# The first product of the dense stage in quarter blocks, one behind each rotating product

## The chip, the cores and the metric

The kernel runs on one core of one Trainium2 chip, as one program and one launch. The metric is the device time of that core in microseconds (us), smaller is better. The engines go by the short names of the profile: PE is the matrix engine (its weight loads are PEld), DVE the vector engine, ACT the scalar engine, POOL the general-purpose engine, SP the engine that only issues DMAs here. Each engine works through its own queue in order. Work on different engines is ordered only by semaphores.

## What is computed

The reference is one encoder layer over 1024 tokens of width 1024: attention beside a convolution, an output product, and then a product-key expert layer with 128 x 128 = 16384 experts, of which each token uses 16 in each of 8 heads. Only that last layer matters here:

```python
u = peer_u[e]                                          # 128 experts of one token
h = jax.nn.gelu(jnp.einsum('cd,chkd->chk', xc, u))
return jnp.einsum('chk,chkd->cd', g * h, peer_v[e])
```

Products are in float32, made of three products each in a shorter format: every operand X is split into a high part (rounded) and a low part (the rest), and X·Y is taken as XhYh + XhYl + XlYh.

## The kernel before

**Two ways through the experts.** Three of the eight token tiles (384 tokens, "gathered") fetch their 768 x 128 expert rows by indirect DMA: one DMA a step (`Gather.issue`, L1147, POOL) brings one row of 1024 numbers to each of 128 tokens, and DVE either forms a dot product with it (phase 0, L1178) or adds it, weighted, to a running sum (phase 1, L1192). There are 768 such steps. The other five tiles (640 tokens, "dense") are multiplied with all 16384 experts, and a dense matrix of gates, zero nearly everywhere, chooses. The dense work goes in 128 blocks of 128 experts.

**A dense block i** has these parts:

- The first product: the block's U (512 KB, `uload`, L1209), split by `usplit` into `uh` on ACT and `ul` on DVE or POOL, times the tokens `HN`. That is 2 halves of 320 tokens, each 8 chunks x 3 = 24 matmuls of 320 columns (`uhalf`, L1479), into one PSUM bank, the tile `hps` (`ubank`). ACT takes the gelu of each half into `ho` (`ugelu`, L1489).
- 33 of the 128 blocks (`US`, index `UI`) have their first product made before the main loop. Their `ho` waits in DRAM (`HDm`) and is read back by `hload` (L1459). They are blocks 0, 1, 2, and then about every fourth. The other 95 blocks make it in the main loop.
- `amake`: DVE multiplies the two halves of `ho` by the gates `gl` (L1466), ACT rounds it to `ah` (L1469), DVE forms `al` (L1471). `gload` (L1442) fetches the gates for four blocks at a time, in two halves, into 3 buffers.
- `vload` (L1446) and `vsplit`: V to `vh` on ACT and `vl` on POOL (L117, L120).
- The second product: 10 output tiles of 128 tokens x 512. Four of them stay in PSUM for all blocks (`acc`, 12 matmuls of 512 columns a block). Six rotate: each is made every second block for two blocks at once (6 matmuls, tile `prot`, one PSUM bank), and DVE adds the bank to `X` (L1514). So a block has three rotations, 18 matmuls. PSUM is full: four banks `acc`, one `hps`, one `prot`, two for the gather's running sum `ga`.

**The order is written out by hand** (a manual schedule), so every engine's queue is in program order. Block i goes: some gather steps, `amake(i+1)`, loads, the four `acc` products, `vsplit(i+1)`, `usplit(i+3)`, and then the rotations. If block i+2 needs its first product (`hasu`), one half of it follows each of the first two rotations: rotation, 24 matmuls, rotation, 24 matmuls, rotation. If it doesn't (a "plain" block), the rotations follow one another, and the second of them borrows the bank `hps`. `wts` and `SPOTS` say how many gather steps a block has and where: a plain block gets 0.3 of the weight of another.

Of the kernel before, what the change touches and what calls it, by code (L numbers as in the profile page):

```python
# [8 lines left out]
F32 = mybir.dt.float32  # L9
# [5 lines left out]
ALU = mybir.AluOpType  # L15
# [5 lines left out]
P = 128  # L21
# [3 lines left out]
DC = D // P  # L25
# [6 lines left out]
NK = 128  # L32
# [6 lines left out]
NG = 3  # L39
# [1 line left out]
GCH = 4  # L41
NPERS = 4
K0 = 33
GW = 0.3
WIN = 2
NVI = 3
NO2 = 2
# [25 lines left out]
def peer_block(tc, I, out):  # L73
# [4 lines left out]
    def f(ap):  # L78
        return ap.bitcast(F32)
# [35 lines left out]
    def split(hi, lo, src, hi_eng=A, lo_eng=V):  # L115
        if hi_eng is A:
            A.copy(hi, src)  # L117
        else:
            hi_eng.tensor_copy(hi, src)
        lo_eng.tensor_tensor(lo, src, f(hi), op=ALU.subtract)  # L120
# [995 lines left out]
    class Gather:  # L1116
        def __init__(self):
            self.seq = [(ph, t, k) for t in range(NG) for ph in (0, 1) for k in range(P)]
            self.ni = self.nc = 0
            self.rows = {}  # L1120
            self.hh, self.aa = {}, {}
            self.limit = NG * 256
            self.slots = None
            self.ps = None
            self.hload = -1

        def h(self, t):
            h = QB[:, 0:2, :].rearrange("p a b -> p (a b)")
            if self.hload < t:
                SY.dma_start(h, HND[t])  # L1130
                self.hload = t
            return h

        def to_psum(self, ps):
            self.ps = ps
# [26 lines left out]
        def adv(self, n=1):  # L1162
            for _ in range(n):
                if not self.ready():
                    return
                self.fill()
                ph, t, k = self.seq[self.nc]
                r = self.rows.pop(self.nc)
                self.nc += 1
                ps = self.ps  # L1170
                if ph == 0:
                    h = self.h(t)
                    if k == 0:
                        self.hh[t] = gp.tile([P, P], F32, name=f"hh{t}")
                        if ps is not None:
                            A.copy(ps, h)
                    jk = QB[:, 2, :].bitcast(BF)
                    V.scalar_tensor_tensor(jk, r, 1.0, h if ps is None else ps, op0=ALU.mult, op1=ALU.mult,  # L1178
                                           accum_out=self.hh[t][:, k:k + 1])
                else:  # L1180
                    if k == 0:
                        aa = gp.tile([P, P], F32, name=f"aa{t}")
                        A.activation(aa[:], self.hh[t][:], AF.Gelu_apprx_tanh)
                        V.tensor_tensor(aa[:], aa[:], gg[t][:], op=ALU.mult)
                        self.aa[t] = aa
                    xt = X[:, t, :]
                    if k == 0 and ps is not None:
                        A.copy(ps, xt)
                    if k == P // 2 and t + 1 < NG:
                        self.h(t + 1)  # L1190
                    to = xt if ps is None else ps
                    V.scalar_tensor_tensor(to, r, self.aa[t][:, k:k + 1], to, op0=ALU.mult, op1=ALU.add)  # L1192
                    if k == P - 1 and ps is not None:
                        A.copy(xt, ps)
                self.slots.append(r)

    gat = Gather()
    US = sorted({0, 1, 2, *(int(2 + j * (NK - 2) / (K0 - 2)) for j in range(K0 - 2))})
# [13 lines left out]
    def HE(i):  # L1212
        return G if i in UI and UI[i] <= KM else A

    def usplit(i):
        raw = RAW.pop(("u", i))
        uh = uu.tile([P, DC, P], F32R, name="uh", tag="uh", bufs=2)
        ul = uu.tile([P, DC, P], F32R, name="ul", tag="ul", bufs=2)
        split(uh[:], ul[:], raw[:], hi_eng=HE(i), lo_eng=(G if UI[i] <= KM else V) if i in UI else G if i % 4 else V)
        UW[i] = (uh, ul)  # L1220

    def useg(i, hps, d0, d1):
# [185 lines left out]
    with ExitStack() as vs:  # L1408
# [40 lines left out]
        def vsplit(i):  # L1449
# [3 lines left out]
            split(vh[:], vl[:], raw[:], lo_eng=G)  # L1453
            CH[i] = (vh, vl)

        def hload(i):
            if i in UI:
                ho = vp.tile([P, TD], F32, name="ho", tag="ho", bufs=2)
                SY.dma_start(ho[:], HDm[UI[i]])  # L1459
                HO[i] = ho  # L1460

        def amake(i, mid=lambda: None):
            ho = HO.pop(i)
            for hf in range(2):
                o = ho[:, hf * HT_:(hf + 1) * HT_].rearrange("p (b t) -> p b t", t=TB)
                V.tensor_tensor(o, o, gl[i - i % GCH, hf][:, :, i % GCH, :], op=ALU.mult)  # L1466
            ah = vp.tile([P, TD], F32R, name="ah", tag="ah", bufs=WIN + 1)
            al = vp.tile([P, TD], F32R, name="al", tag="al", bufs=WIN + 1)
            A.copy(ah[:], ho[:])  # L1469
            mid()  # L1470
            V.tensor_tensor(al[:], ho[:], f(ah[:]), op=ALU.subtract)  # L1471
            AL[i] = (ah, al)

        def uhalf(i, hf, ps, d0=0, d1=DC):
            a, b = segs[hf]
# [12 lines left out]
            a, b = segs[hf]  # L1488
            A.activation(ho[:, a:b], ps[:, :b - a], AF.Gelu_apprx_tanh)  # L1489

        def loads(i, u):
            if 0 <= u < NK and u not in UI:
                uload(u)
            if 0 <= i < NK:
                if i % GCH == 0:
                    gload(i)
                hload(i)
                vload(i)

        last = [-1] * len(rot)  # L1500
        HP = {}
# [16 lines left out]
        gat.to_psum(ga[:])  # L1518
        for i in range(KM + 2, K0):
            uload(US[i])  # L1520
        loads(-1, 3)
        loads(0, -1)
        loads(1, -1)
        for i in range(KM, K0):
            if i + 1 < K0:
                usplit(US[i + 1])
            else:
                amake(0)
                vsplit(0)
            ho = vp.tile([P, TD], F32, name="hm", tag="al", bufs=WIN + 1)[:]  # L1530
            for hf in range(2):
                hps = ubank() if hf == 0 else psv.tile([P, 512], F32, name="prot", tag="r", bufs=1)
                uhalf(US[i], hf, hps)
                ugelu(ho, hf, hps)
            SY.dma_start(HDm[i], ho)

        def uof(i):
            return i + 2 < NK and i + 2 not in UI


        SPOTS = {True: (4, 3, 1, 4, 3, 2, 0, 4), False: (1, 2, 0)}
        gat0 = gat.nc
        wts = np.cumsum([(1.0 if uof(i) else GW) * (i < NK - GLAST) for i in range(NK)])
        for i in range(NK):
            nx = i + 1
            hasu = uof(i)
            ng = gat0 + int(np.ceil((ngat - gat0) * wts[i] / wts[-1])) - gat.nc
            gs = [0] * 6
            for j in range(ng):
                gs[SPOTS[hasu][j % len(SPOTS[hasu])]] += 1  # L1550
            if nx in HP:
                ugelu(HO[nx], 1, HP.pop(nx))
            gat.adv(gs[0])
            if nx < NK:
                amake(nx, lambda: gat.adv(gs[1]))
            else:
                gat.adv(gs[1])
            gat.adv(gs[2])
            loads(i + 2, i + 4)
            ah, al, vh, vl = *AL[i], *CH[i]  # L1560
            for j, (t, n) in enumerate(pers):
                mm3(acc[j][:], ah[:, t * P:(t + 1) * P], al[:, t * P:(t + 1) * P], vh[:, n:n + 512],
                    vl[:, n:n + 512], i == 0, i == NK - 1)
            if nx == NK:
                gat.adv(10000)
                gf = gat.slots.pop(0)
                SY.dma_start(gf, row("final_g"))
                for t in range(NG):
                    final(t)
                for j, (t, n) in enumerate(pers):  # L1570
                    V.tensor_tensor(X[:, NG + t, n:n + 512], X[:, NG + t, n:n + 512], acc[j][:], op=ALU.add)
                    if n:
                        final(NG + t)
            if nx < NK:
                vsplit(nx)
            if i + 3 < NK and i + 3 not in UI:
                usplit(i + 3)
            rs_ = [w for w in range(len(rot)) if i % WIN == w % WIN or i == NK - 1]
            if hasu:
                HO[i + 2] = vp.tile([P, TD], F32, name="ho", tag="ho", bufs=2)  # L1580
            for j, w in enumerate(rs_):
                rotate(w, i, not hasu and j % 2 == 1)
                if nx == NK and rot[w][1]:
                    final(NG + rot[w][0])
                gat.adv(gs[3 + j] if 3 + j < 6 else 0)
                if hasu and j < 2:
                    hps = ubank()
                    uhalf(i + 2, j, hps)
                    if j == 0:
                        ugelu(HO[i + 2], 0, hps)  # L1590
                    else:
                        HP[i + 2] = hps
            gat.adv(sum(gs[3 + len(rs_):]))
            CH.pop(i - WIN, None)
        while fq:
            final2()
    h_.close()
# [55 lines left out]
```

## Time and profile before

| | |
|---|---|
| median of three runs | 3069.0 us (3067.18 to 3072.01) |
| the profiled execution, its own time | 3063.84 us |
| span of the profiled execution | 3062.0 us |
| PE busy | 2807.3 us, 92% of the span |
| DVE / POOL / ACT busy | 2425.7 / 1901.2 / 1152.5 us (79 / 62 / 38%) |
| DMA, mean | 232 GB/s over the span; 323 GB/s from 1384 to 3037 us |

The page of the profile gives totals over the whole span. The dense loop, which the change touches, runs from the first matmul of block 0 (1384.04 us) to the first of block 127 (3036.99 us), a little over half of the span. A matmul's duration in the rows is longer than its share of the engine, because matmuls are pipelined. The pitch, from one start to the next, is what a matmul costs.

### The profile page before, as it was taken

The numbers are of one execution on the slowest core, as the hardware profiler recorded it, in microseconds if no ns is written. First come the engines' busy times: TensorE is split into PE (matmuls) and PEld (weight loads), VectorE is DVE, ScalarE is ACT, GpSimd is POOL, SyncE is SP. The second block draws the span as 40 slices with busy tenths as digits, with TensorE's granted clock in tenths as the row PEclk, the third lists the DMA queues.
The fourth block names the chain that finished last, engine by engine and source line by source line (L and its number), as shares of the span: only waits on it lengthen the run. The fifth ranks groups of instructions, "written<-read, shape, count | busy, mean of one in ns | idle before, by whom it ended". The sixth has DMA issues, their size and how long they took to land.

```text
span 3062.0 us, 44586 instructions
## 1 busy us (share of the span) xinstructions
PE 2807.3 (92%) x16048; PEld 2491.3 (81%) x16048; DVE 2425.7 (79%) x4496; ACT 1152.5 (38%) x2376; POOL 1901.2 (62%) x1526
## 2 busy tenths in 40 slices
PE   7878899799999999979999999999999999999998
PEld 6767788698988888858888888888888888888887
DVE  5889997458666977658888888888888888788877
ACT  3216565243577677662222222222222222222222
POOL 2578852105446666747777777777767676767765
PEclk8989999899999999989999999999999999999999
DMA  3111000153345666678989898989999898889985
GB/s 124 48 67 35 8 1 15 44 159 118 97 146 191 210 232 248 223 262 331 337 326 345 320 338 318 340 330 334 345 317 325 302 339 306 316 314 323 331 296 217
DMA packets 296719, 710.32 MB, mean 232 GB/s; under 512 B 25265, under 2 KB 135217, under 8 KB 296369
## 3 DMA queue, kind: packets, MB, share of 16 engines
q0 software_dynamic: 110592, 402.70, 35.7%
q1 hardware_dynamic: 156800, 252.85, 24.5%
q10 hardware_dynamic: 29104, 51.91, 4.5%
q8 instruction: 126, 2.06, 0.3%
q14 instruction: 97, 0.79, 0.1%
HBM read 640.46 MB, written 66.91 MB: 231 GB/s over the span
## 4 chain that ended last, share of the span: by engine, by line
PE 65%; DVE 19%; issue 6%; ACT 4%; DMA 3%; POOL 1%; ACTq 1%; SPq 0%; POOLq 0%; DVEq 0%
PE hps L1479 19%; PE prot L123 5%; PE hps L1227 5%; PE prot L124 5%; PE prot L125 5%; PE acc L123 3%; PE acc L124 3%; PE acc L125 3%; DVE y L147 3%; PE pg L1099 3%; DVE ul L120 2%; DVE QB L1178 2%; DVE ga L1192 1%; DVE ho L1466 1%; PE pq L282 1%
## 5 line engine op out<-in xcount | busy, mean ns | idle before, releaser
L1479 PE MATMUL hps<-HN,uh 128*128 128x320 f32 x3072 | 679.6, 309 | 5.4 <-ACT ho L1234 5.3
L1479 PEld LDWEIGHTS hps<-HN,uh 128*128 128x128 f32 x3072 | 522.7, 188 | 21.2 <-issue 5.5
L1147 POOL DMA_INDIRECT rows<-peer_u,ei x339 | 369.4, 1090 | 194.3 <-DVE QB L1178 126.9
L1479 PE MATMUL hps<-HN,ul 128*128 128x320 f32 x1536 | 475.3, 309 | 0.0
L1147 POOL DMA_INDIRECT rows<-peer_v,ei x329 | 339.2, 1031 | 216.3 <-DVE ga L1192 146.3
L1514 DVE TENSOR_TENSOR X<-X,prot 128x512 f32<-128x512 f32 x352 | 241.0, 685 | 238.1 <-PE prot L125 236.6
L1192 DVE SCALAR_TENSOR_TENSOR ga<-rows,aa,ga 128x1024 f32<-128x1024 f32 x329 | 422.4, 1284 | 5.2 <-DMA rows<-peer_v,ei 1.2
L123 PE MATMUL prot<-vh,ah 128*128 128x512 f32 x699 | 282.7, 404 | 84.3 <-DVE X L1514 84.1
L1489 ACT ACTIVATE ho<-hps 128x320 f32<-128x320 f32 x190 | 83.1, 437 | 728.0 <-PE hps L1479 728.0
L120 POOL TENSOR_TENSOR vl<-vr,vh 128x1024 fp32r<-128x1024 f32 x128 | 309.1, 2415 | 56.0 <-DMA vr<-peer_v 36.6
L1178 DVE SCALAR_TENSOR_TENSOR QB<-rows,ga 128x1024 bf16<-128x1024 f32 x271 | 329.4, 1216 | 5.6 <-DMA rows<-peer_u,ei 1.7
L1469 ACT CAST ah<-ho 128x640 fp32r<-128x640 f32 x128 | 93.3, 729 | 521.3 <-DVE ho L1466 307.6
L1479 PEld LDWEIGHTS hps<-HN,ul 128*128 128x128 f32 x1536 | 289.1, 188 | 0.0
L124 PE MATMUL prot<-vl,ah 128*128 128x512 f32 x699 | 277.9, 398 | 0.0
L125 PE MATMUL prot<-vh,al 128*128 128x512 f32 x699 | 276.5, 396 | 0.0
L120 POOL TENSOR_TENSOR ul<-ur,uh 128x1024 fp32r<-128x1024 f32 x96 | 240.2, 2503 | 2.6
L123 PEld LDWEIGHTS prot<-vh,ah 128*128 128x128 f32 x699 | 132.9, 190 | 121.0 <-DVE X L1514 100.1
L1109 ACT COPY gblk<-pg 128x128 f32<-128x128 f32 x640 | 175.6, 439 | 99.2 <-PE pg L1099 71.2
L1227 PE MATMUL hps<-HN,uh 128*128 128x320 f32 x992 | 210.5, 334 | 0.0
L124 PE MATMUL acc<-vl,ah 128*128 128x512 f32 x512 | 205.1, 401 | 3.4 <-POOL vl L120 3.4
L123 PE MATMUL acc<-vh,ah 128*128 128x512 f32 x512 | 206.1, 403 | 0.0
L125 PE MATMUL acc<-vh,al 128*128 128x512 f32 x512 | 203.9, 398 | 0.0
(265 smaller groups left out, 6672.9 us busy)
## 6 DMA issues: line engine op xcount, KB each, us to landing
ur<-peer_uT SPq DMA_DIRECT2D x128, 512.0 KB, 4.9
vr<-peer_v SPq DMA_DIRECT2D x128, 512.0 KB, 6.4
GD<-gblk ACTq DMA_DIRECT2D x80, 512.0 KB, 4.9
gl<-GD SPq DMA_DIRECT2D x64, 640.0 KB, 8.0
wqr<-peer_wq SPq DMA_DIRECT2D x32, 512.0 KB, 3.9
ho<-HDm SPq DMA_DIRECT2D x33, 320.0 KB, 6.3
HDm<-ho SPq DMA_DIRECT2D x31, 320.0 KB, 2.3
s<-SD SPq DMA_DIRECT2D x64, 128.0 KB, 2.4
```

What stands on the lines that cost most here:

```text
L120: lo_eng.tensor_tensor(lo, src, f(hi), op=ALU.subtract)
L123: PE.matmul(ps, ah, bh, start=start, stop=False)
L124: PE.matmul(ps, ah, bl, start=False, stop=False)
L125: PE.matmul(ps, al, bh, start=False, stop=stop)
L1109: A.copy(gblk[b][k][:, :, q * 4:q * 4 + 4].rearrange("p i t -> p t i"), pg[:, :, k * w:k * w + w])
L1147: G.indirect_dma_start(out=r, out_offset=None, in_=I["peer_v" if ph else "peer_u"], in_offset=bass.IndirectOffsetOnAxis(ap=ge[t][:, k:k + ...
L1178: V.scalar_tensor_tensor(jk, r, 1.0, h if ps is None else ps, op0=ALU.mult, op1=ALU.mult, accum_out=self.hh[t][:, k:k + 1])
L1192: V.scalar_tensor_tensor(to, r, self.aa[t][:, k:k + 1], to, op0=ALU.mult, op1=ALU.add)
L1227: PE.matmul(hps[:, j, :b - a], (uh, uh, ul)[st3][:, dc, :], HN[(0, 1, 0)[st3]][:, dc, a:b], start=dc == 0 and st3 == 0, stop=dc == DC - 1 ...
L1469: A.copy(ah[:], ho[:])
L1479: PE.matmul(ps[:, :b - a], (uh, uh, ul)[st3][:, dc, :], HN[(0, 1, 0)[st3]][:, dc, a:b], start=dc == 0 and st3 == 0, stop=dc == DC - 1 and ...
L1514: V.tensor_tensor(X[:, NG + t, n:n + 512], X[:, NG + t, n:n + 512], pr, op=ALU.add)
```

## The change

In the loop, the first products no longer belong to block i+2. A list `ulist` of the 95 blocks that need one is worked off in quarters: `ugroup` makes 4 of the 8 chunks of one half (12 matmuls of 320 columns), and one `ugroup` follows every rotation of every block. So 127 blocks with three each hold the 95 x 4 = 380 quarters. The gelu comes behind every second quarter. `uahead` splits a block's U ahead and issues the load of the one two further on. The four `acc` products are spread: one behind the first rotation, one behind the second, two behind the third. Every rotation uses `prot`; none borrows `hps`.

`amake` is cut into `amake1` (gates and `ah`) and `amake2` (`al`), and stands behind the second quarter instead of at the head of the block, with a share of the gather steps between. The gather steps are spread evenly, 5 or 6 in each block. `vsplit(i+1)` stands at the head of the block. In `usplit` all low parts but those of the first products ahead of the loop go to POOL; before, 31 of them in the loop went to DVE. `ho` gets three explicit buffers, of which one is the space `QB` that held the gather's token row; that row is loaded into a gather slot instead (`stage`), four steps ahead of its use. The last block stands behind the loop.

```diff
+        def stage(self, t):
+            if t not in self.staged:
+                self.staged[t] = self.slots.pop(0)
+                SY.dma_start(self.staged[t], HND[t])
...
-        split(uh[:], ul[:], raw[:], hi_eng=HE(i), lo_eng=(G if UI[i] <= KM else V) if i in UI else G if i % 4 else V)
+        split(uh[:], ul[:], raw[:], hi_eng=HE(i), lo_eng=V if i in UI and UI[i] > KM else G)
...
+        hfree = [vp.tile([P, TD], F32, name=f"ho{j}")[:] for j in range(2)]
+        hfree.append(QB[:, 0:2, :].rearrange("p a b -> p (a b)")[:, :TD])
...
+        def uahead():
+            m = ug["g"] // 4
+            if ug["split"] < min(m + 2, len(ulist)):
+                usplit(ulist[ug["split"]])
+                ug["split"] += 1
+                if ug["load"] < len(ulist):
+                    uload(ulist[ug["load"]])
+                    ug["load"] += 1
+
+        def ugroup():
+            m, q = divmod(ug["g"], 4)
...
+            i, (hf, d) = ulist[m], divmod(q, 2)
...
+            if d == 0:
+                ug["ps"] = ubank()
+            uhalf(i, hf, ug["ps"], d * DC // 2, (d + 1) * DC // 2)
+            if d == 1:
+                if hf == 0:
+                    HO[i] = hfree.pop(0)
+                ugelu(HO[i], hf, ug["ps"])
+            ug["g"] += 1
...
-            gat.adv(gs[0])
-            if nx < NK:
-                amake(nx, lambda: gat.adv(gs[1]))
...
-            loads(i + 2, i + 4)
...
+        SPOTS = (0, 2, 1, 0, 2, 2, 0)
...
+            hload(nx)
+            if len(hfree) > 1:
+                hload(i + 2)
+            loads(i + 2)
+            vsplit(nx)
+            uahead()
+            rs_ = [w for w in range(len(rot)) if i % WIN == w % WIN]
+            rotate(rs_[0], i, False)
+            accum(i, (0,))
+            ugroup()
+            gat.adv(gs[0])
+            rotate(rs_[1], i, False)
+            accum(i, (1,))
+            ugroup()
+            uready(nx)
+            amake1(nx)
+            gat.adv(gs[1])
+            amake2(nx)
+            rotate(rs_[2], i, False)
+            accum(i, (2, 3))
+            ugroup()
+            gat.adv(gs[2])
```

## Rows read from the trace of the kernel before

**Rows 1.** The page's chain of work that ended last, its shares of the span by engine.

```profile
PE 65%; DVE 19%; issue 6%; ACT 4%; DMA 3%; POOL 1%; ACTq 1%; SPq 0%; POOLq 0%; DVEq 0%
```

**Rows 2.** Busy time by stretch: the dense loop from the first matmul of block 0 to the first of block 127 (stretch, length, then busy us and instructions of PE, PEld, DVE, ACT, POOL, then the granted clock of PE as a share of full speed, the DMA share and GB/s), and under it two stretches of 100 us.

```profile
1384.04:3036.99 1652.95, 1569.91 (x8363) 1395.76 (x8362) 1393.20 (x1809) 395.73 (x552) 1176.50 (x886) 0.98 0.90 323
...
1700.00:1800.00 100.00, 95.33 (x519) 85.10 (x518) 86.11 (x92) 24.38 (x34) 71.74 (x56) 1.00 0.93 338
2900.00:3000.00 100.00, 94.06 (x482) 83.17 (x481) 80.72 (x86) 22.28 (x31) 67.46 (x50) 0.93 0.86 306
```

**Rows 3.** The timeline of PE in the dense loop (start us, duration us, engine, line, operation, names, count; in brackets the idle time before and what ended it): a block with a first product begins at 2255.68, the next block, a plain one, at 2269.57, and the one behind it at 2279.62.

```profile
2255.68 0.39 PE L123 MATMUL acc<-vh,ah 128*128 128x512 f32 x1
...
2259.76 0.45 PE L1479 MATMUL hps<-HN,uh 128*128 128x320 f32 x2
...
2260.20 0.46 PE L1479 MATMUL hps<-HN,uh 128*128 128x320 f32 x2
...
2269.57 0.39 PE L123 MATMUL acc<-vh,ah 128*128 128x512 f32 x1
...
2278.14 0.50 PE L123 MATMUL prot<-vh,ah 128*128 128x512 f32 x1 [2.97 <-DVE X L1514]
...
2279.62 0.40 PE L123 MATMUL acc<-vh,ah 128*128 128x512 f32 x1
```

**Rows 4.** What PE waited for in the dense loop (us in total, times, longest).

```profile
PE prot L123 <- DVE X L1514: 81.3, 33, 3.0
```

**Rows 5.** The timeline of DVE, and under it of POOL, across that plain block's idle stretch.

```profile
2274.29 3.19 DVE L120 TENSOR_TENSOR ul<-ur,uh 128x1024 fp32r<-128x1024 f32 x1
2277.41 0.68 DVE L1514 TENSOR_TENSOR X<-X,prot 128x512 f32<-128x512 f32 x1
2278.00 0.67 DVE L1514 TENSOR_TENSOR X<-X,hps 128x512 f32<-128x512 f32 x1
...
2274.01 2.38 POOL L120 TENSOR_TENSOR vl<-vr,vh 128x1024 fp32r<-128x1024 f32 x1
```

**Rows 6.** The timeline of PE behind another plain block's idle stretch.

```profile
2225.84 0.63 PE L123 MATMUL prot<-vh,ah 128*128 128x512 f32 x1
2226.26 0.63 PE L124 MATMUL prot<-vl,ah 128*128 128x512 f32 x1
```

**Rows 7.** Groups by line on DVE from 1386.6 to 3052 us (count, then busy us, mean ns of one, and the idle time before them with what ended it).

```profile
L1192 DVE SCALAR_TENSOR_TENSOR ga<-rows,aa,ga 128x1024 f32<-128x1024 f32 x329 | 422.4, 1284 | 5.2 <-DMA rows<-peer_v,ei 1.2 <-ACT ga L1188 0.5
L1178 DVE SCALAR_TENSOR_TENSOR QB<-rows,ga 128x1024 bf16<-128x1024 f32 x269 | 327.0, 1216 | 5.6 <-DMA rows<-peer_u,ei 1.7 <-ACT ga L1176 1.4
...
L1466 DVE TENSOR_TENSOR ho<-ho,gl 128x320 f32<-128x320 f32 x252 | 123.5, 531 | 2.4 <-DMA ho<-HDm 2.4
L1471 DVE TENSOR_TENSOR al<-ho,ah 128x640 fp32r<-128x640 f32 x126 | 103.1, 818 | 0.0
L120 DVE TENSOR_TENSOR ul<-ur,uh 128x1024 fp32r<-128x1024 f32 x31 | 101.6, 3279 | 0.0
L1192 DVE SCALAR_TENSOR_TENSOR ga<-rx,aa,ga 128x1024 f32<-128x1024 f32 x55 | 70.6, 1283 | 0.4
L1178 DVE SCALAR_TENSOR_TENSOR QB<-rx,ga 128x1024 bf16<-128x1024 f32 x45 | 54.7, 1216 | 3.6 <-DMA rx<-peer_u,ei 1.8 <-ACT ga L1176 1.4
```

**Rows 8.** One group by line on POOL in the same stretch, and the timeline of POOL: two gather steps with nothing between, and one beside a two-input operation of DVE.

```profile
L120 POOL TENSOR_TENSOR ul<-ur,uh 128x1024 fp32r<-128x1024 f32 x64 | 154.5, 2413 | 0.0
...
2266.42 0.95 POOL L1147 DMA_INDIRECT rows<-peer_v,ei  x1 [0.30 <-issue]
2267.68 0.94 POOL L1147 DMA_INDIRECT rows<-peer_v,ei  x1 [0.30 <-issue]
...
2272.73 1.27 POOL L1147 DMA_INDIRECT rows<-peer_v,ei  x1 [2.87 <-DVE ga L1192]
```

**Rows 9.** The timeline of DVE, and under it of POOL, at the start of the dense stage: two-input operations of DVE alone and beside a split on POOL.

```profile
1370.08 1.23 DVE L120 TENSOR_TENSOR ul<-ur,uh 128x1024 fp32r<-128x1024 f32 x1 [26.16 <-ACT uh L117]
...
1382.14 1.93 DVE L1466 TENSOR_TENSOR ho<-ho,gl 128x320 f32<-128x320 f32 x1
...
1381.32 2.41 POOL L120 TENSOR_TENSOR vl<-vr,vh 128x1024 fp32r<-128x1024 f32 x1 [36.59 <-DMA vr<-peer_v]
```

**Rows 10.** The timeline of SP behind a load of gates, what SP's queue waited for with that load, and the DMA view of one issue of `vr` each at 1664.47 and at 1871.07 (count, size, us from issue to landing).

```profile
1664.47 1.24 SPq L1446 DMA_DIRECT2D vr<-peer_v  x1
...
SPq L1442 <- DVE ho L1466: 302.6, 31, 15.8
...
vr<-peer_v SPq DMA_DIRECT2D x1, 512.0 KB, 7.1
...
vr<-peer_v SPq DMA_DIRECT2D x1, 512.0 KB, 10.6
```

**Rows 11.** The timeline of ACT in the dense loop.

```profile
1563.89 1.05 ACT L117 CAST vh<-vr 128x1024 fp32r<-128x1024 f32 x1
1564.84 1.04 ACT L117 CAST uh<-ur 128x1024 fp32r<-128x1024 f32 x1
1568.07 0.44 ACT L1489 ACTIVATE ho<-hps 128x320 f32<-128x320 f32 x1 [2.20 <-PE hps L1479]
```

**Rows 12.** The DMA view from 1400 to 3030 us (issues, KB each, median us to landing).

```profile
QB<-HND SPq DMA_DIRECT2D x2, 512.0 KB, 7.8
```

**Rows 13.** The timeline of PE at the end: the first matmul of block 127.

```profile
3036.99 0.40 PE L123 MATMUL acc<-vh,ah 128*128 128x512 f32 x1
```

More of the change, by code (lines that the diff above doesn't have):

```diff
@@ L43 @@
 K0 = 33
-GW = 0.3
 WIN = 2
@@ L1125, in __init__ @@
             self.hload = -1
+            self.staged = {}
         def h(self, t):
@@ L1171, in adv @@
                 if ph == 0:
-                    h = self.h(t)
+                    h = self.h(t) if ps is None else ps
                     if k == 0:
@@ L1175, in adv @@
                         if ps is not None:
-                            A.copy(ps, h)
+                            self.stage(t)
+                            A.copy(ps, self.staged[t])
+                            self.slots.append(self.staged.pop(t))
                     jk = QB[:, 2, :].bitcast(BF)
-                    V.scalar_tensor_tensor(jk, r, 1.0, h if ps is None else ps, op0=ALU.mult, op1=ALU.mult,
+                    V.scalar_tensor_tensor(jk, r, 1.0, h, op0=ALU.mult, op1=ALU.mult,
                                            accum_out=self.hh[t][:, k:k + 1])
@@ L1188, in adv @@
                         A.copy(ps, xt)
-                    if k == P // 2 and t + 1 < NG:
-                        self.h(t + 1)
                     to = xt if ps is None else ps
@@ L1195, in adv @@
                 self.slots.append(r)
+                if ph and k == P - 4 and t + 1 < NG and ps is not None:
+                    self.stage(t + 1)
     gat = Gather()
@@ L1454, in vsplit, with amake1 @@
             CH[i] = (vh, vl)
+        hfree = [vp.tile([P, TD], F32, name=f"ho{j}")[:] for j in range(2)]
+        hfree.append(QB[:, 0:2, :].rearrange("p a b -> p (a b)")[:, :TD])
         def hload(i):
[L1457 to L1463, printed above, removed]
+            if i in UI and i not in HO and i < NK:
+                HO[i] = hfree.pop(0)
+                SY.dma_start(HO[i], HDm[UI[i]])
+        def amake1(i):
+            ho = HO[i]
             for hf in range(2):
@@ L1467, in amake, with amake2 @@
             ah = vp.tile([P, TD], F32R, name="ah", tag="ah", bufs=WIN + 1)
+            A.copy(ah[:], ho)
+            AL[i] = ah
+        def amake2(i):
+            ho = HO.pop(i)
             al = vp.tile([P, TD], F32R, name="al", tag="al", bufs=WIN + 1)
[L1469 to L1472, printed above, removed]
+            V.tensor_tensor(al[:], ho, f(AL[i][:]), op=ALU.subtract)
+            AL[i] = (AL[i], al)
+            hfree.append(ho)
         def uhalf(i, hf, ps, d0=0, d1=DC):
@@ L1489, in ugelu, with loads @@
             A.activation(ho[:, a:b], ps[:, :b - a], AF.Gelu_apprx_tanh)
-        def loads(i, u):
-            if 0 <= u < NK and u not in UI:
-                uload(u)
+        def loads(i):
             if 0 <= i < NK:
@@ L1496, in loads, with uready @@
                     gload(i)
-                hload(i)
                 vload(i)
+        ulist = [i for i in range(NK) if i not in UI]
+        ug = dict(g=0, split=0, load=0, ps=None)
+        def uahead():
[8 more added lines that the diff above has]
+            m, q = divmod(ug["g"], 4)
+            if m >= len(ulist):
+                return
+            i, (hf, d) = ulist[m], divmod(q, 2)
+            if ug["split"] <= m:
+                uahead()
[4 more added lines that the diff above has]
+                if hf == 0:
+                    HO[i] = hfree.pop(0)
+                ugelu(HO[i], hf, ug["ps"])
+            ug["g"] += 1
+        def uready(i):
+            while i not in UI and ulist.index(i) >= ug["g"] // 4:
+                ugroup()
         last = [-1] * len(rot)
@@ L1520, in peer_block @@
             uload(US[i])
-        loads(-1, 3)
-        loads(0, -1)
-        loads(1, -1)
+        for j in range(2):
+            uload(ulist[j])
+        ug["load"] = 2
+        hload(0)
+        loads(0)
+        loads(1)
         for i in range(KM, K0):
@@ L1527, in peer_block @@
             else:
-                amake(0)
+                amake1(0)
+                amake2(0)
                 vsplit(0)
+                uahead()
             ho = vp.tile([P, TD], F32, name="hm", tag="al", bufs=WIN + 1)[:]
@@ L1535, in peer_block, with accum @@
             SY.dma_start(HDm[i], ho)
[L1537 to L1552, printed above, removed]
-            gat.adv(gs[0])
-            if nx < NK:
-                amake(nx, lambda: gat.adv(gs[1]))
-            else:
-                gat.adv(gs[1])
-            gat.adv(gs[2])
-            loads(i + 2, i + 4)
+        def accum(i, js):
@@ L1560, in peer_block @@
             ah, al, vh, vl = *AL[i], *CH[i]
-            for j, (t, n) in enumerate(pers):
+            for j in js:
+                t, n = pers[j]
                 mm3(acc[j][:], ah[:, t * P:(t + 1) * P], al[:, t * P:(t + 1) * P], vh[:, n:n + 512],
                     vl[:, n:n + 512], i == 0, i == NK - 1)
[L1564 to L1592, printed above, removed]
@@ L1593, in peer_block @@
-            gat.adv(sum(gs[3 + len(rs_):]))
-            CH.pop(i - WIN, None)
+        SPOTS = (0, 2, 1, 0, 2, 2, 0)
+        gat0 = gat.nc
+        nb = NK - GLAST
+        for i in range(NK - 1):
+            nx = i + 1
+            ng = gat0 + -(-(ngat - gat0) * min(nx, nb) // nb) - gat.nc
+            gs = [0] * 3
+            for j in range(ng):
+                gs[SPOTS[j % len(SPOTS)]] += 1
+            hload(nx)
[3 more added lines that the diff above has]
+            vsplit(nx)
+            uahead()
+            rs_ = [w for w in range(len(rot)) if i % WIN == w % WIN]
[12 more added lines that the diff above has]
+            accum(i, (2, 3))
+            ugroup()
+            gat.adv(gs[2])
+            CH.pop(i - WIN, None)
@@ new lines, in peer_block @@
+        accum(NK - 1, range(len(pers)))
+        gat.adv(10000)
+        gf = gat.slots.pop(0)
+        SY.dma_start(gf, row("final_g"))
+        for t in range(NG):
+            final(t)
+        for j, (t, n) in enumerate(pers):
+            V.tensor_tensor(X[:, NG + t, n:n + 512], X[:, NG + t, n:n + 512], acc[j][:], op=ALU.add)
+            if n:
+                final(NG + t)
+        for w in range(len(rot)):
+            rotate(w, NK - 1, w % 2 == 1)
+            if rot[w][1]:
+                final(NG + rot[w][0])
```

## The prediction

> **What bounds the kernel now.** I read the chain of waits first: PE holds 65% of it, DVE 19% [rows 1]. Busy time by stretch then shows that the dense loop is the place: there PE is busy 1569.91 of 1652.95 us, DVE 1393, POOL 1177, and the DMA engines stand at 0.90 [rows 2]. No engine is full, so I looked for where PE stands idle. In PE's timeline a block with a first product takes 2269.57 − 2255.68 = 13.89 us without a gap; the plain block behind it takes 10.05 us, of which 2.97 are idle [rows 3]. The list of waits says that this is the pattern: PE waits for DVE's add to X 33 times, 81.3 us in all [rows 4]. DVE's timeline says why the add is late: a `ul` of 3.19 us stands ahead of it [rows 5]. So PE bounds 95 blocks of the loop, and DVE the plain ones.
>
> How much can be won? The price of a matmul is its pitch. Three of 320 columns take 2260.20 − 2259.76 = 0.44 us, so one takes 0.1467 and a first product 48 × 0.1467 = 7.04. The rest of the full block, 30 matmuls of 512 columns, takes 13.89 − 7.04 = 6.85, or 0.2283 each [rows 3]. Up to the start of block 127 the loop has 127 × 12 `acc` matmuls, 127 × 9 of the rotations that last ran in block 126, and 126 × 9 of the others: 3801. So PE needs 3801 × 0.2283 + 95 × 7.04 = 867.8 + 668.8 = 1536.6 us, against 1652.95: **116.4 us can be won at most**. Of these 81.3 are the waits [rows 4]. Most of the rest is the clock: behind an idle stretch the pitch is 2226.26 − 2225.84 = 0.42 us in place of 0.23 [rows 6], PE then being at the lower of its two levels (1.2, not 2.4 GHz), and the granted clock falls from 1.00 to 0.93 late in the loop [rows 2].
>
> **The change, part by part.**
>
> *Quarters on PE.* PE's work stays; every block now has 30 × 0.2283 + 36 × 0.1467 = 12.13 us of it, nearly evenly: 2.44 us between the first two rotations (3 + 12 matmuls) and between the next two, 3.13 (6 + 12) between the third and the next block. The one bank `prot` must be added within that time. PE's next rotation began 2278.14 − 2277.41 = 0.73 after the start of the add that it waited for [rows 3, 5]. DVE sees the last matmul some 0.2 us after its slot (an estimate: its 0.39 less the pitch of 0.23 [rows 3]). So an add may start 2.44 − 0.73 − 0.2 = 1.5 us late without PE noticing.
>
> *DVE.* There are 329 + 269 + 55 + 45 = 698 gather steps, 5.5 a block, at about 1.3 us (1284 ns, or 1216 and the reading of the accumulator) [rows 7]. An add has a pitch of 0.60 for its duration of 0.68 [rows 5]; with the same 0.09 off, a block has three adds 1.80, two `ho` 0.80, one `al` 0.73 [rows 7] and 7.15 of gathering: 10.5 us of 12.13. Between the rotations this is 0.60 + 2.6 against PE's 3.81, then 0.60 + 0.80 + 1.3 + 0.73 = 3.4 against 3.81, then 0.60 + 2.6 or 3.9 against 4.50. Every stretch fits. In even blocks a gelu, behind the second quarter, stands ahead of `ah` on ACT and holds `al` back some 1.2 us; that lies within the 1.5. The 31 `ul` that leave DVE free 101.6 us there [rows 7]. So the 81.3 us of waits go, and with them the low clock: nothing else holds PE for 3 us at a time. Late next would be an add behind the three gather steps of a six-step block; that is 4.5 us of DVE against 4.50 of PE, no later than it was.
>
> *POOL.* It takes those 31 `ul` at 2413 ns [rows 8], +74.8 us on 1177 of 1537: no wait of its own if the order allows. Per four blocks it has 7 splits × 2.42 = 16.9, 22 gather steps at the pitch 2267.68 − 2266.42 = 1.26, 27.7, and some 0.33 (1.27 in place of 0.94) for eight that meet a two-input operation of DVE, 2.6 [rows 8]: **47.2 of 48.5 us**. That is tight, but rows are fetched seven ahead, and `vl` is now made a block ahead.
>
> *Two-input operations.* `ul` on DVE takes 1.23 us alone, 3.19 beside a POOL split; a half of `ho` that met one took 1.93 and ended with it (1381.32 + 2.41 = 1383.73) [rows 5, 9]. In the new order POOL splits from about 1 to 6 us into a block, and `amake1` comes behind two rotations, a gap and an add, at 1.37 + 2.44 + 1.37 + 0.8 = 6.0: they touch now and then. I take 0.5 us a block, which DVE's slack of 1.6 covers; the bounds are 0 and a whole split, 2.4, for each.
>
> The Trainium skill ("SBUF — State Buffer", section "Who interferes with whom") says that a DVE instruction with two SBUF inputs contends with a POOL instruction that reads SBUF, under an exclusive lock held for the whole instruction. By that rule the trace agrees (1.93 against about 0.45, ending with the split), and each `ul` moved to POOL lengthens the time in which `ho` and `al` can be shut out; the third rival below is what it would make of that.
>
> *A new wait.* SP's queue: in one block of four, `gload` fetches four blocks' gates; its second half needs the buffer that `amake1` of the last block of the old four reads, and SP's queue stood 31 times, 302.6 us, for DVE's `ho` there [rows 10]. That is now 6.4 us into the block (`amake1` at 6.0, one half 0.4), and `vload` is queued behind it, issued at about 7.1. Of eight such issues of `vr` behind a gate load, four landed near the least, 7.1 us, and four near the most, 10.6 [rows 10]. So V comes 2.1 to 5.6 us into the next block, where `vsplit` now stands at the head: ACT waits with `vh`, and behind it are `uh` and then the gelu of the first quarter. `vh` and `uh` have a pitch of 0.95 each, the gelu takes 0.44 [rows 11], so it ends at 4.5 to 8.0. PE wants the bank `hps` for the next half at 3.81 + 2.05 = 5.86. The stall is 0 to 2.1 us, 1.0 in the mean, in 31 blocks: **31 us** (bounds 0 and 65).
>
> *Start, end, staging.* At the start SP waits with a second `uload` until DVE's `ul`, which ends at 1371.3 [rows 9]; the loads of block 0 follow. I take +1.5 us (0 to 3). In block 126 the last gelu comes just in time, and the chain gelu, `ho`, `ah`, `al` is 1.2 us longer than PE's cover. The gather's token row, staged four steps (9 us) ahead, against a landing of 7.8 [rows 12], costs nothing, or twice 2 us if late. The end behind block 127's start, 3062.0 − 3036.99 = 25.0 [rows 13], has the same work.
>
> **The sum.** 1384.04 + 1.5 + 1536.6 + 31 + 1.2 + 25.0 = 2979.3 us of span. The profiled execution took 1.84 more than its span, 3063.84, and the median of the runs is 5.2 above that. So 2979.3 + 1.8 + 5.2 = **2986 us**, 2.7% faster.
>
> **The rivals.**
>
> *No stall for V.* If `vr` lands near 7.1 us each time, the 31 us go: 2955. The even traffic speaks for it, the eight landings against.
>
> *POOL or the DMA engines become the bound.* If POOL also idles 3 to 4 us in every fourth block for V, its 47.2 become 50.7, above PE's 48.5: 2.2 × 127/4 = 70 us in place of the 31, 3025. The DMA engines have 0.90 × 1653 = 1488 us of work; if they can't hold more than the 0.93 of the busiest 100 us I looked at [rows 2], the loop takes 1600, +63: 3018.
>
> *Slower: POOL's splits shut DVE out.* DVE has 10.5 us a block, and the loop before gave 1652.95/127 = 13.0. If its two-input operations wait more than 2.5 us a block, it is slower than before. Two meetings a block at 3.19 − 1.23 = 2.0 make 14.5, +1.5 × 127 = 190: 3259. For it: with `ul` on POOL in three blocks of four, splits fill 35% of the time. Against: before, `al` met none (818 ns in the mean for 640 columns, where 1.23 us for 1024 give 0.77) and `ho` few (mean 531) [rows 7, 9].
>
> *It doesn't take the waits away.* If adds come late anyway, since each has 2.4 us where a full block gave 3.5, PE waits 0.9 us a block and all is as before: 3069.
>
> **Chances.** Forecast 0.55, no stall 0.15, POOL or DMA 0.18, slower 0.08, nothing won 0.04. A measurement here tells about 0.2%, 6 us, from no change. Faster 0.88, same 0.04, slower 0.08. The range goes from no stall and no start cost (2950) past POOL's case to 3040.
>
> **What would show it.** PE's wait for the add falls from 81.3 us to under 15; its clock is 1.00 throughout; blocks follow at 12.1 us, with a step of about 1 us in each fourth; ACT waits for `vr`, and PE for the gelu, some 31 times; POOL is busy 75 us more in the loop, DVE 100 less; mean of `ho` under 0.9 us. I am wrong if DVE waits for rows, if `ho` takes over a microsecond in the mean, or if PE waits for `vl` or `ul`.

## The result, and the profile after

| | median | runs | range |
|---|---|---|---|
| before | 3070.28 us | 4 | 3067.18 to 3072.01 |
| after | 3001.38 us | 4 | 2998.95 to 3005.17 |

The ratio is 0.9778, with a 95% interval of 0.9761 to 0.9795: 2.2% faster. The forecast was 2986, with a range of 2950 to 3040. The profiled execution took 3001.72 us, its span 2999.9.

After's page: the slices of the granted clock, and the shares of the chain that ended last.

```profile
PEclk9999999999999999999999999999999999999999
...
PE 50%; DVE 21%; DMA 12%; issue 8%; POOL 4%; ACT 4%; ACTq 1%; SPq 0%; POOLq 0%; DVEq 0%
```

After's busy time by stretch: the loop, from the first matmul of block 0 to the first of block 127. The columns are those of [rows 2].

```profile
1387.70:2971.08 1583.38, 1558.32 (x8361) 1380.92 (x8362) 1429.11 (x1778) 388.65 (x548) 1230.71 (x918) 1.00 0.91 337
```

What after's engines waited for between 1387 and 2930 us (us in total, times, longest), answering to [rows 4].

```profile
ACT vh L116 <- DMA vr<-peer_v: 193.3, 31, 7.8
...
PEld prot L122 <- DVE X L1557: 35.3, 63, 1.7
DVE QB L1185 <- DMA rows<-peer_u,ei: 25.8, 32, 2.2
...
PE prot L122 <- DVE X L1557: 18.3, 45, 1.4
DVE ga L1197 <- DMA rows<-peer_v,ei: 16.7, 21, 2.1
...
PE hps L1492 <- ACT QB L1502: 3.4, 3, 1.8
...
PE hps L1492 <- ACT ho L1502: 1.1, 2, 0.7
```

The first of these in the kernel before, from 1384 to 3036 us:

```profile
ACT vh L117 <- DMA vr<-peer_v: 0.2, 1, 0.2
```

After's groups by line on DVE between 1387 and 2935 us: the two halves of `amake1`, of which a third of the blocks use the tile `QB` for `ho`. They answer to L1466 in [rows 7].

```profile
L1475 DVE TENSOR_TENSOR ho<-ho,gl 128x320 f32<-128x320 f32 x166 | 164.9, 1033 | 2.7 <-DMA ho<-HDm 2.7
...
L1475 DVE TENSOR_TENSOR QB<-QB,gl 128x320 f32<-128x320 f32 x82 | 85.1, 1077 | 0.0
```

**How to read it.** The granted clock of the loop is 1.00 where it was 0.98 [rows 2], and PE's wait for the add has gone from 81.3 us, with 3.0 at the longest [rows 4], to 18.3, with 1.4. The loop is 1652.95 − 1583.38 = 69.6 us shorter. It is also 46.8 us over the 1536.6 that the prediction gave as PE's floor. Three things in the views are new. ACT waits 31 times, 193 us, for V, where it waited once, 0.2 us. DVE waits for gathered rows, which it hardly did before [rows 7]. And a gate product takes 1.03 to 1.08 us in the mean, where it took 0.53 [rows 7]: 250 us in all against 123.5. That eats the 101.6 us that DVE was to gain, so DVE is busy 1429 us in the loop, more than before.

Where PE lost its time I worked out from its timeline: each matmul that starts more than 0.08 us later than the pitch allows. In the loop 63 rotations come late behind the add. They lose 29.4 us, and 8.0 more in the slower pitch of the first matmul behind each. In 9 places PE waits for the gelu's bank, 6.0 us. By the block's number modulo 4 the late rotations fall 42 times into blocks 0 and 19 times into blocks 1, and the bank waits all into blocks 3. A block lasts 12.87, 12.37, 12.18 and 12.51 us in the mean for 0, 1, 2 and 3; the shortest lasts 12.11.

One such place can be followed in the timelines of after, engine by engine: SP; ACT; POOL; DVE; PE.

```profile
2248.57 22.25 SPq L1449 DMA_DIRECT2D gl<-GD  x2
2270.91 0.58 SPq L1453 DMA_DIRECT2D vr<-peer_v  x1
...
2278.92 1.05 ACT L116 CAST vh<-vr 128x1024 fp32r<-128x1024 f32 x1 [6.40 <-DMA vr<-peer_v]
...
2280.83 0.42 ACT L1502 ACTIVATE ho<-hps 128x320 f32<-128x320 f32 x1
...
2280.05 2.41 POOL L119 TENSOR_TENSOR vl<-vr,vh 128x1024 fp32r<-128x1024 f32 x1 [2.14 <-ACT vh L116]
2282.42 2.66 POOL L119 TENSOR_TENSOR ul<-ur,uh 128x1024 fp32r<-128x1024 f32 x1
...
2294.27 2.41 POOL L119 TENSOR_TENSOR ul<-ur,uh 128x1024 fp32r<-128x1024 f32 x1
...
2281.78 3.65 DVE L1475 TENSOR_TENSOR ho<-ho,gl 128x320 f32<-128x320 f32 x2
...
2294.26 3.18 DVE L1475 TENSOR_TENSOR ho<-ho,gl 128x320 f32<-128x320 f32 x2
...
2307.28 1.29 DVE L1197 SCALAR_TENSOR_TENSOR ga<-rows,aa,ga 128x1024 f32<-128x1024 f32 x1 [1.31 <-DMA rows<-peer_v,ei]
...
2281.65 0.45 PE L1492 MATMUL hps<-HN,uh 128*128 128x320 f32 x2
...
2304.45 0.50 PE L122 MATMUL prot<-vh,ah 128*128 128x512 f32 x1 [0.22 <-DVE X L1557]
...
2309.22 0.50 PE L122 MATMUL prot<-vh,ah 128*128 128x512 f32 x1 [0.70 <-DVE X L1557]
```

SP's second load of gates stands for 21.4 us (the line takes both loads together) and holds back the `vr` behind it, which is issued at 2270.91 and lands 8 us later. Block 71 began at 2275.77; its `vh` comes 3.15 us in. POOL, which does its splits in program order, does `vl` at 2280.05 and `ul` at 2282.42, and the two gate products of DVE meet both: 3.65 us in place of some 0.9. POOL's gather steps stand behind the splits, so POOL is late in block 72, from 2288.00, as well: its `ul` starts at 2294.27, within 0.01 us of DVE's `ho` at 2294.26, of which two take 3.18. The rows that POOL issues behind come late too: DVE waits 1.31 us for one at 2307.28, in block 73, its add comes late, and PE's rotation at 2309.22 waits 0.70.

### The profile page after: what moved, and what is told of

The parts are those of the page before. It is cut to its first block, busy times and chain, and to the rows that moved or that the text cites. A ratio compares the mean times of both kernels' runs of the same rounds, so it can differ in the third digit from the quotient of the medians.

```text
span 2999.9 us, 44538 instructions
## 1 busy us (share of the span) xinstructions
PE 2796.1 (93%) x16048; PEld 2476.5 (83%) x16048; DVE 2464.3 (82%) x4465; ACT 1148.3 (38%) x2376; POOL 1951.2 (65%) x1557
## 4 chain that ended last, share of the span: by engine, by line
PE 50%; DVE 21%; DMA 12%; issue 8%; POOL 4%; ACT 4%; ACTq 1%; SPq 0%; POOLq 0%; DVEq 0%
PE hps L1492 12%; PE hps L1234 5%; PE prot L122 4%; PE prot L123 3%; PE prot L124 3%; DMA rows<-peer_u,ei 3%; DMA vr<-peer_v 3%; DVE y L146 3%; PE pg L1098 3%; DMA rows<-peer_v,ei 3%; DVE ga L1197 2%; PE acc L122 2%; PE acc L124 2%; PE acc L123 2%; DVE ho L1475 2%
## 5 line engine op out<-in xcount | busy, mean ns | idle before, releaser
L1197 DVE SCALAR_TENSOR_TENSOR ga<-rows,aa,ga 128x1024 f32<-128x1024 f32 x330 | 423.9, 1285 | 23.3 <-DMA rows<-peer_v,ei 16.7
L1152 POOL DMA_INDIRECT rows<-peer_u,ei x339 | 360.3, 1063 | 109.5 <-issue 57.9
L119 POOL TENSOR_TENSOR vl<-vr,vh 128x1024 fp32r<-128x1024 f32 x128 | 308.9, 2413 | 154.0 <-ACT vh L116 110.8
L1152 POOL DMA_INDIRECT rows<-peer_v,ei x330 | 325.4, 986 | 110.6 <-issue 64.1
L1185 DVE SCALAR_TENSOR_TENSOR QB<-rows,ga 128x1024 bf16<-128x1024 f32 x271 | 329.5, 1216 | 30.0 <-DMA rows<-peer_u,ei 25.8
L122 PE MATMUL prot<-vh,ah 128*128 128x512 f32 x762 | 308.3, 405 | 29.2 <-DVE X L1557 26.9
L119 POOL TENSOR_TENSOR ul<-ur,uh 128x1024 fp32r<-128x1024 f32 x127 | 323.2, 2545 | 2.6
L1557 DVE TENSOR_TENSOR X<-X,prot 128x512 f32<-128x512 f32 x384 | 262.0, 682 | 68.1 <-PE prot L124 66.7
L123 PE MATMUL prot<-vl,ah 128*128 128x512 f32 x762 | 301.2, 395 | 0.4 <-POOL vl L119 0.4
L124 PE MATMUL prot<-vh,al 128*128 128x512 f32 x762 | 297.6, 390 | 0.0
L1502 ACT ACTIVATE ho<-hps 128x320 f32<-128x320 f32 x128 | 55.8, 436 | 486.4 <-PE hps L1492 486.4
L116 ACT CAST vh<-vr 128x1024 fp32r<-128x1024 f32 x128 | 133.7, 1045 | 202.1 <-DMA vr<-peer_v 193.3
L122 PEld LDWEIGHTS prot<-vh,ah 128*128 128x128 f32 x762 | 143.3, 188 | 64.6 <-DVE X L1557 44.5
```

Of the source, the lines that this page charges most:

```text
L122: PE.matmul(ps, ah, bh, start=start, stop=False)
L123: PE.matmul(ps, ah, bl, start=False, stop=False)
L124: PE.matmul(ps, al, bh, start=False, stop=stop)
L1152: G.indirect_dma_start(out=r, out_offset=None, in_=I["peer_v" if ph else "peer_u"], in_offset=bass.IndirectOffsetOnAxis(ap=ge[t][:, k:k + ...
L1185: V.scalar_tensor_tensor(jk, r, 1.0, h, op0=ALU.mult, op1=ALU.mult, accum_out=self.hh[t][:, k:k + 1])
```

## The experiments

The theory after this reading was that the late V costs nearly all of the 46.8 us, not through the gelu's bank, as the prediction had it, but by shifting POOL's splits onto DVE's products. The rivals: the loss lies in the quarter order itself (an add has too little room); or the gain comes from the 31 `ul` alone, whatever the order. Two batches were run, each beside runs of before (3067.72 and 3068.48 us).

### V ahead of the gates

```diff
         def loads(i):
             if 0 <= i < NK:
+                vload(i)
                 if i % GCH == 0:
                     gload(i)
-                vload(i)
```

> The changed kernel with the load of V issued ahead of the load of gates in SP's queue, so that V no longer waits behind the gate buffer. Theory A (late V in each fourth block pushes POOL's two splits into the time of amake1, DVE's ho then waits for them, and the adds come late): ACT's 193 us of waits for vr fall under 60, the mean of ho from 1.02 us to under 0.7, PE's late rotations from 63 to under 30, and the time falls by 20 to 35 us to 2966 to 2981. Rival B (seven splits in four blocks meet ho anyway, whenever V comes): the waits for vr go too, but ho stays near 1.0 us and the time within 6 us of 3001.

Measured: 2965.26 us (2963.45 to 2968.5), ratio 0.9672 [0.9652, 0.9692]. Its busy time by stretch, over the same loop:

```profile
1387.20:2932.38 1545.18, 1541.05 (x8362) 1382.14 (x8362) 1324.18 (x1778) 385.36 (x548) 1238.36 (x918) 1.00 0.92 345
```

Its waits between 1387 and 2930 us:

```profile
PE prot L122 <- DVE X L1557: 4.0, 5, 1.1
ACT vh L116 <- DMA vr<-peer_v: 0.4, 1, 0.4
```

Its group of gate products on DVE:

```profile
L1475 DVE TENSOR_TENSOR ho<-ho,gl 128x320 f32<-128x320 f32 x170 | 93.0, 586 | 4.9 <-DMA ho<-HDm 3.1 <-ACT ho L1502 1.8
```

The order of two DMA issues on SP is worth 36 us of median and 38.2 of the loop. (By the ratios, each kernel beside its own runs of before, it is 0.0106 of 3069, 33 us; the differences to after that are told below as medians differ from those by the ratios by 1 to 5 us.) All three signs go together: the wait for V (193.3 to 0.4), the long products (1033 to 586 ns), the waits for rows (25.8 and 16.7 to 8.4 and 6.0). Late rotations fall from 63 to 5. POOL's and PE's timelines show the shift itself: over 30 rounds, `vl` and `ul` start 4.5 and 6.8 us into blocks 3 in the mean in after, and 1.5 and 3.8 with V first; in blocks 0 it is 4.3 and 6.6 against 1.8 and 4.2. The gate products start 6.0 us in at the earliest. The loop is now 8.6 us over the floor of 1536.6. So the quarter order itself has room enough.

### The 31 `ul` back on DVE

```diff
-        split(..., lo_eng=V if i in UI and UI[i] > KM else G)
+        split(..., lo_eng=(G if UI[i] <= KM else V) if i in UI else G if i % 4 else V)
```

> The changed kernel with the old rule for the low part of U: every fourth block's ul goes back from POOL to DVE, all else as changed. Theory A (DVE is the engine with no room, 1.6 us a block): some 24 ul of 1.2 to 3.2 us each, 30 to 75 us of DVE, of which a third to a half reaches PE: 3015 to 3040. Rival B (POOL is the engine that is late; relieving it of a sixth of its splits ends the meetings with ho): 2980 to 3000.

Measured: 3030.7 us (3028.08 to 3034.94), ratio 0.9878 [0.9854, 0.9902]. Here the first add of a block with such an `ul` is late 32 times, 49.1 us, and those blocks last 14.23 us in the mean. It is 29 us slower than after, but still 37 faster than before: with this `ul` left on DVE, the rest of the change gains by itself.

### Only the one line, in the kernel before

```diff
-        split(..., lo_eng=(G if UI[i] <= KM else V) if i in UI else G if i % 4 else V)
+        split(..., lo_eng=V if i in UI and UI[i] > KM else G)
```

> The kernel before with only the new rule for the low part of U: all ul of the loop on POOL, no quarters, nothing else moved. Theory A (the quarters and the even gather are what ends the waits of plain blocks): the add is still late there, for three rotations follow one another: PE's waits stay above 50 us and the time at 3045 to 3069. Rival C (the 3.2 us ul ahead of the add was the whole of it): PE's 81 us of waits fall under 25, the clock stays at 1.00, and the time is 2985 to 3010, as low as with the whole change.

Measured: 2962.52 us (2958.06 to 2969.63), ratio 0.9667 [0.9642, 0.9692]. Busy time by stretch:

```profile
1385.07:2932.52 1547.45, 1540.42 (x8363) 1378.65 (x8362) 1308.18 (x1778) 396.33 (x552) 1220.92 (x918) 1.00 0.93 345
```

PE's wait for the add (L1514 in this kernel) and ACT's wait for V:

```profile
PE prot L123 <- DVE X L1514: 3.8, 6, 1.2
...
ACT vh L117 <- DMA vr<-peer_v: 4.5, 6, 1.2
```

This is the finding of the study: one of the change's many lines, in the old order, takes the 81.3 us of waits [rows 4] to 3.8 and the clock to 1.00. It beats the whole change by 39 us, or 34 by the ratios. It can't be told from after with V first (2958 to 2970 against 2963 to 2969).

### The four `acc` products together again

```diff
+            accum(i, range(4))
             rotate(rs_[0], i, False)
-            accum(i, (0,))
...
-            accum(i, (1,))
...
-            accum(i, (2, 3))
```

> The changed kernel with the four acc products together at the head of the block, so that only a quarter (12 matmuls, 1.76 us) stands between two rotations in place of 2.44 or 3.13. Theory A (what counts is the room for one bank's add, which falls from 1.5 to 0.8 us): every block waits some 0.3 to 0.5 us, 40 to 60 us more, 3040 to 3060. Rival B (adds are late only behind a ho that waited for a split, by a microsecond or more, and small room does not matter): 3001 to 3015.

Measured: 3046.65 us (3034.79 to 3066.51), ratio 0.9928 [0.9903, 0.9954]. The profiled execution is the longest of the five, 3066.51. Its waits between 1392 and 3002 us:

```profile
ACT vh L116 <- DMA vr<-peer_v: 248.8, 31, 14.0
...
PE hps L1492 <- ACT ho L1502: 27.2, 17, 6.6
...
PE hps L1492 <- ACT QB L1502: 19.4, 9, 7.1
...
PE acc L124 <- DVE al L1483: 12.5, 33, 0.4
```

The experiment was to shorten the room of an add, but the adds are late in only some 16 places, 8.5 us. What grew is the door that the prediction had named: the gelu behind the late `vh` and `uh` makes PE wait for the bank, 30 times and 51.6 us by PE's timeline, all in blocks 3, which last 14.90 us from first rotation to first rotation. Besides, the `acc` products, now first in the block, come late behind `al` 33 times, some 18 us by PE's timeline; in after PE never waited there. With the `acc` products in front, the quarters of a block lie closer together, and the bank is wanted sooner.

The same with V first, as above:

> The acc products together at the head of the block and V loaded ahead of the gates. Theory A (what the acc order cost was the late gelu of every fourth block: 52 us at the bank hps, not the smaller room for the adds): with V in time it costs nothing, 2962 to 2975, hps waits under 10 us. Rival B (the smaller room costs by itself): late adds show in all blocks, 2985 to 3020.

Measured: 2968.84 us (2962.73 to 2970.5), ratio 0.9684 [0.9663, 0.9704]; the gate products take 496 and 490 ns, the waits for the bank 0.3 us in all, and two adds are late. So where the `acc` products stand makes no difference that can be told (3.6 us, with ranges that overlap) as long as V is in time. Their spreading softened the late V, no more.

### Gate products with one input

```diff
-                o = ho[:, hf * HT_:(hf + 1) * HT_].rearrange("p (b t) -> p b t", t=TB)
-                V.tensor_tensor(o, o, gl[i - i % GCH, hf][:, :, i % GCH, :], op=ALU.mult)
+                o = small.tile([P, NB2], F32, name="ss10")
+                V.tensor_reduce(o[:], gl[i - i % GCH, hf][:, :, i % GCH, :], axis=AX.X, op=ALU.add)
```

> The changed kernel, V still late, but in amake1 the two products of ho with the gates are replaced by two reductions of the gates (one input in SBUF, 320 elements each, nearly the same DVE time): the gates are left out of the result, all loads, buffers and waits for the gates stay. Theory A (the late splits reach PE through the two-input ho alone): ACT still waits some 31 times, about 190 us, for vr; the reductions take about 0.45 us each with none long; late rotations fall from 63 to under 20; time 2966 to 2982. Rival B (late V reaches PE by gather rows issued late behind the splits, and by the gelu's bank): waits for rows and late rotations stay, 2988 to 3002.

Measured: 2980.25 us (2976.05 to 2983.28), ratio 0.9717 [0.9695, 0.9739]. Its group in place of the products (the gates have no part in the result here):

```profile
L1475 DVE TENSOR_REDUCE ss<-gl 128x10 f32<-128x320 f32 x252 | 109.8, 477 | 0.0
```

Its waits:

```profile
ACT vh L116 <- DMA vr<-peer_v: 176.6, 32, 9.4
...
DVE QB L1185 <- DMA rows<-peer_u,ei: 39.7, 29, 3.2
DVE ga L1197 <- DMA rows<-peer_v,ei: 31.6, 28, 2.8
PE prot L122 <- DVE X L1557: 14.1, 12, 2.5
```

V is nearly as late as in after, and POOL's `ul` of blocks 3 still starts 6.0 us in (mean), where the reductions stand, but none of the 252 reductions is long: they take 473 to 483 ns. By "SBUF — State Buffer", section "Who interferes with whom", of the Trainium skill, a DVE instruction with at most one SBUF input, outside the two-port modes, does not contend with POOL, and on trn2 a reduction never does. The trace agrees (483 ns at the most, beside 3.65 us for two products in after). With the meetings gone the kernel is 21 us faster than after, of the 36 that V in time gives. The edit also lets `ah` start without waiting for DVE, but that doesn't seem to be the gain: DVE waited 15.0 us for `ah` in after and 42.6 here. The rest is read as coming through POOL itself: its gather steps still stand behind late splits, and DVE's waits for rows grow to 39.7 and 31.6 us.

### The `ul` back, with V first

Both edits above, made together.

> The quarters with the old rule for the low part of U (31 on DVE) and V loaded ahead of the gates. Theory A (of the 29 us that the old rule costs the changed kernel, the wait of ul on DVE in the first block of four is its own, 49 us at the second rotation; V's part goes): 3000 to 3020. Rival B (both come from POOL being late; with V in time ul on DVE meets no split and takes 1.2 us): 2962 to 2980.

Measured: 3047.56 us (3042.73 to 3050.83), ratio 0.9933 [0.9911, 0.9955]. This missed: I expected 3000 to 3020, since the late V would no longer cost anything. It is 17 us slower than with the late V. Its group of the `ul` on DVE, from 1387 to 2935 us:

```profile
L119 DVE TENSOR_TENSOR ul<-ur,uh 128x1024 fp32r<-128x1024 f32 x30 | 79.6, 2654 | 41.2 <-ACT uh L116 41.2
```

With V late, the same group has a mean of 1745 ns, and 6.2 us of waiting for `uh`. V in time brings POOL's `vl` to where DVE's `ul` stands, at the head of the block, and DVE stands there for ACT's `uh`, too. By the two timelines every one of these `ul` runs beside a `vl` and takes 2.39 us or more; with V late 24 of 30 take 1.22 or 1.23, and six take 3.45 to 4.04. So the same `ul`, on the same engine, takes 0.9 us more in the mean by when POOL's `vl` starts. The first add of those blocks is late 31 times, 63.3 us.

### The two ends

After with V first (as above), the gather steps spread so that they end one block earlier (`GLAST = 2`), and at the start the gates and V ahead of the second U:

```diff
-GLAST = 1
+GLAST = 2
...
-        for j in range(2):
-            uload(ulist[j])
+        uload(ulist[0])
         ug["load"] = 2
         hload(0)
-        loads(0)
-        loads(1)
+        gload(0)
+        vload(0)
+        vload(1)
+        uload(ulist[1])
```

> V loaded ahead of the gates, and the two ends of the loop mended: the second uload behind the loads of blocks 0 and 1 at the start, and the gather steps finished one block sooner (GLAST 2). Theory: block 0 starts 1 to 2 us sooner and the end behind block 127's start takes 25 in place of 29 us: 2957 to 2962, 0 to 8 us under V first alone. Rival: the denser gather steps (5.54 a block) or the later U cost what the ends give: 2965 to 2970.

Measured: 2954.93 us (2953.24 to 2958.07), ratio 0.9639 [0.9621, 0.9657]; the fastest of the study, and faster than both kernels. Block 0 starts at 1386.49 (1387.20 with V first alone), the loop takes 1543.3 (1545.2), and the end behind block 127's start 23.4 us (29.3). So most of the gain (5.9 of 8.5 us of span) is the end. In after, PE and DVE show why:

```profile
2971.08 0.39 PE L122 MATMUL acc<-vh,ah 128*128 128x512 f32 x1
...
2984.33 0.79 PE L122 MATMUL prot<-vh,ah 128*128 128x512 f32 x1 [8.24 <-DVE X L1557]
...
2971.94 2.61 DVE L1197 SCALAR_TENSOR_TENSOR ga<-rows,aa,ga 128x1024 f32<-128x1024 f32 x2
```

The last two gather steps end 3.5 us behind the start of block 127, the closing work of the tokens waits for them, and PE stands idle for 8 us.

**The table of both factors** (medians):

| | `ul` on DVE and POOL | `ul` on POOL |
|---|---|---|
| order of before | 3068 | 2962.5 |
| quarters | 3030.7 | 3001.4 |
| quarters, V first | 3047.6 | 2965.3 |

The quarters gain 37 us while part of the `ul` stands on DVE, and none once all of it is on POOL.

## Why the prediction came out as it did

**What held.** The two places to win from were named rightly: PE's waits for the add behind DVE's `ul` and the low clock they bring. Both went, and with V in time the loop is within 11 us of the floor of 1536.6 worked out from pitches (1545.2, 1547.5 and 1543.3 in three kernels). The new wait was seen, with its count of 31 and its mechanism on SP's queue. POOL's rise was 1230.7 − 1176.5 = 54 us rather than 75. Neither POOL nor the DMA engines became the bound: with V first the loop had a DMA share of 0.92 at 345 GB/s, and e3's went to 0.93.

**The step that failed** is "Two-input operations", and with it the price of "A new wait". The prediction took 0.5 us a block for meetings of `ho` with POOL's splits and let DVE's slack of 1.6 us cover it. It priced the late V apart from that, at the gelu's bank, 31 us. In fact the two are one thing. The late V moves POOL's splits to where `amake1` stands, 6.0 us into the block: in block 71 `vl` starts 2255.17 − 2252.99 = 2.2 us in with V first, and 2280.05 − 2275.77 = 4.3 in after (POOL's and PE's timelines). By DVE's timeline the products' excess over 0.45 us is 86.1 us in blocks 3, 48.6 in blocks 0 and 7.6 in blocks 2: over 31 rounds that is 4.3 us in two neighbouring blocks, against 3.2 of slack, while a mean over all blocks (1.1 us) still lies under the 1.6. A mean hid what a phase decides. The bank itself cost 6.0 us; late adds with their restarts cost 37.4. The bank was sized too high because the landings were: half of the prediction's eight took near 10.6 us, while of after's 31 `vr` behind the gates 27 landed within 8.4 us (7.3 to 10.2). So in block 71 the gelu ends 5.5 us in (2280.83 + 0.42 − 2275.77), and PE wants the bank at 5.9 (2281.65), as predicted. That the total came near is in part luck: 31 us were put down for the late V, and 36 were found, on another path. The one-input run shows that the meetings carry about 21 of the 36 us, and rows issued late behind the shifted splits are left as the reading of the rest; that they are all of it was not tested by itself.

**The sum, term by term.** Start of the loop: +3.66 us (1387.70 for 1384.04) where I took 1.5. Loop: 1583.4 where the terms gave 1536.6 + 31 + 1.2 = 1568.8, so 14.6 too little. End: 2999.9 − 2971.08 = 28.8 where I took 25.0; "the same work" it was, but the last gather steps came later against block 127. Together 20.6 us over the span of 2979.3; the median stood 1.5 above the span, where I took 7.0, which leaves 15 on the time.

**Its own signs.** The wait for the add (18.3, "under 15"), the clock (1.00), ACT's 31 waits for `vr`: as said, or nearly. PE waited for the gelu 9 times, not some 31, and the longest blocks were 0 (12.87 us), not only each fourth one with the late V (12.51). "DVE 100 less" was wrong by sign (+36). Of the signs it gave for being wrong, two appeared: `ho` over a microsecond in the mean, and DVE waiting for rows. They were the right ones to name. PE waited for `vl` once, 0.4 us, and for `ul` once, 0.6.

**The rivals.** "No stall for V" gave 2955 for a `vr` that lands early; with V issued early it is 2965. "Slower: POOL's splits shut DVE out" had the right mechanism and decided from 2.5 us a block; it reached 1.0: products and `al` took 126 us more than before in 124 blocks (their groups against [rows 7]). "It doesn't take the waits away" fell.

**What it never asked** is what each part is worth alone. It gave the quarters their share in ending the waits, because plain blocks were where PE stood idle. But the rows already pointed to what e3 shows: the add in [rows 5] stood behind one `ul` of 3.19 us, in a block whose PE idles 2.97 [rows 3]. The quarter order brought nothing on top, and the late V that came with it cost 36 us. The gates stood ahead of V in SP's queue before, too, but there `amake` stood at the head of the block and `vsplit` behind the four `acc` products, and ACT waited 0.2 us for V in all.

## What to carry to other kernels

When waits are traced to one instruction on the wrong engine, move that instruction by itself first, and reorder only what is then still late. In a queue that works in order, ask of every instruction that can stand (here a load whose buffer is still read) what is behind it, and put the urgent one ahead. Where one engine's work holds up another's, lay out the phases of both within the block; a mean of the collisions per block says nothing on whether slack covers them.

## What was not expected of the hardware

A gate product takes 0.48 us when POOL doesn't split (2966.71 and 1381.70 in after's timeline: 0.48 and 0.49), and up to 3.65 for two beside POOL's splits, while reductions of the same 128x320 at the same place take 473 to 487 ns all along. `ul` on DVE had means of 3279 ns [rows 7], 1745 and 2654 in three orders of the same work, against 1.23 us alone [rows 9]. POOL's own splits hardly suffer: `vl` took 2415 ns before and 2413 after, `ul` 2413 [rows 8] and 2483.
